# Expert stage of a hybrid transformer block: last products of a pair over all four column runs at once, 8 KB weight rows, sums in fours, gather steps behind the activation's product

## The chip, the cores and the metric

One core of a Trainium2 chip runs one program. The metric is the device time of one execution in microseconds (us); the kernel before takes 2264.77 us (median of 3 runs, 2264.67 to 2266.06).

## The reference, cut to what matters

One layer: a mixing part (convolution, neighbourhood attention, a gated recurrence), then a mixture of experts (MoE), then a norm. The change is in the MoE: 512 tokens, each sent to 2 of 32 experts, each expert with three weight matrices of 4 MiB in fp32.

```python
def _hier_moe(h, w_rg, b_rg, w_re, b_re, w1, w3, w2):
    ...
    def expert_block(args):
        e, xb = args
        return (jax.nn.silu(xb @ w1[e]) * (xb @ w3[e])) @ w2[e]

    ys = lax.map(expert_block, (blk_e, xs)).reshape(P, D)
    ys = ys * slot_w.astype(ys.dtype)[:, None]
    return jax.ops.segment_sum(ys, slot_tok, num_segments=N + 1)[:N]
```

With D = 2048 and 512 hidden columns, w1 and w3 are 2048 x 512 and w2 is 512 x 2048.

## The kernel before

The experts run in 16 **pairs** (`expert_pair`, L1444). An expert has 64 token slots, so that the two experts j of a pair stand side by side in the array: a product takes 64 of the 128 columns of TensorE (PE) for each of them, and the results fill the two halves of one PSUM bank. A fp32 matmul of the program is two rows MATMUL in the profile. Two pairs make a **group** of four experts: the first pair of a group has e divisible by 4, the second has e % 4 = 2.

A pair goes through these steps.

- `w1`, then `w3` (L1449 to L1463): four chunks c of 32 matmuls in all for each matrix, into a bank of `held`. After a chunk come other pieces of work: `run(late, 2)` after the first three chunks of w1, and `steps(...)` by the table `STEPS` (L43): in a second pair after each chunk of w3, in a first pair after the first two of w1.
- After w1, SiLU on ScalarE (ACT, L1467), a small product `pa` with slots and weights of the tokens (L1473), and the one-hot matrix `oht` on VectorE (DVE, L1482).
- After w3, DVE multiplies the two results (L1484), PE transposes (`pt`, L1488), ACT copies them out (`at`, L1490).
- The last products with w2 (`down_two`, L1511), for two column runs of 512 at a time: c = 0, 1 into `held[0:2]`, then c = 2, 3 into two banks `pd`; the weights come as tiles of 1024 columns, for each expert 4 KB of a row.
- DVE scales a run's result (`ys`, L1508), and `split` makes two parts of it (`wh` by ACT L128, `wl` by DVE L129).
- The **sums** (`combine`, L1426): for each column run c and each block t of 128 tokens two matmuls with all 128 columns (`pc<-wh`, `pc<-wl`, L1433), then one add on DVE into the output `xf` (L1440). They stand as separate pieces, one t each, in the queue `late`, and 16 pieces are run between later products, one or two at a time.

A **gather step** (L1387 to L1408) is a part of the next group's input: eight matmuls (L1398, `parts` with the one-hot `oh`), then the next input's part on ACT (L1246) and DVE (L1249); after every fourth step four activations on ACT write `hg` (L1406) out of two banks, `held[2:]`.

Every engine runs its instructions in the order in which the program emits them (the kernel is under a manual schedule), so that the order of the calls sets what waits behind what. The 8 PSUM banks are four `held` and four of the pool `bg`, from which `pc`, `pa`, `pt` and `pd` come. Weights are loaded by SyncE's queue into places of 1 MiB, as soon as a place is free (`load_weights`, L1149).

```python
STEPS = {"w3": (2, 2, 2, 2), "w2": (2, 2), "w1": (2, 2, 0, 0)}
...
        nc.vector.tensor_mul(a, gu[1], a)
        run(late, 1)
        pt = bank("pt")
        for f in range(4):
            nc.tensor.transpose(pt[:, cc(f)], a[:, cc(f)], ident)
        at = slab.tile([P, 512], F32, name="at", tag="raw", bufs=6)
        nc.scalar.copy(at, pt)
        run(late, 1)
```

Of the kernel before, what the change touches and what calls it, by code (L numbers as in the profile page):

```python
# [39 lines left out]
JOB = {"gate": 0.7, "zf": 1.4, "zb": 1.4, "k": 2.2, "q": 1.4}  # L40
NW = 6
SPLITS = {0: (4,), 1: (5,), 2: (6, 7), 4: (8,), 5: (9,), 6: (10, 11), 8: (12,), 9: (13,), 10: (14,), 11: (15,)}
STEPS = {"w3": (2, 2, 2, 2), "w2": (2, 2), "w1": (2, 2, 0, 0)}  # L43
FIRST = (6, 4, 4, 2)
BOTH = ("k", "v", "zf", "zb", "i")
HEAD = ("zf", "zb", "i", "hq", "g")
# [4 lines left out]
def hybrid_block_kernel(ctx: ExitStack, tc: tile.TileContext, I, out):  # L51
# [10 lines left out]
    def bank(name):  # L62
        return psum.tile([P, 512], F32, name=name, tag="bg")
# [58 lines left out]
    def split(w, n=512, scale=None):  # L122
        wh, wl = split_tiles(n)
        if scale:
            nc.scalar.mul(wh, w, scale)
            nc.vector.scalar_tensor_tensor(wl, w, scale, wh.bitcast(F32), op0=ALU.mult, op1=ALU.subtract)
        else:
            nc.scalar.copy(wh, w)  # L128
            nc.vector.tensor_sub(wl, w, wh.bitcast(F32))  # L129
        return wh, wl  # L130


    cs = work.tile([P, KT, 32], F32, name="cs", tag="bias", bufs=2)
# [103 lines left out]
    def run(q, n):  # L237
        for _ in range(min(n, len(q))):
            q.popleft()()
# [872 lines left out]
    wseq = deque()  # L1112

    def add(name, e, k, nk, o, n):
        v = I[name][e:e + 2].rearrange("e (k p) n -> p e k n", p=P)
        wseq.append((nk, n, v[:, :, k:k + nk, o:o + n]))
# [5 lines left out]
    for e in range(0, NE, 2):  # L1122
        for name in ("w1", "w3"):
            for c in range(4):
                for j in range(2):
                    add_run(name, e + j, c)
        if e < NE - 2:
            for c in (0, 2):
                for k in range(4):
                    add("w2", e, k, 1, 512 * c, 1024)  # L1130
            continue
        for c in range(4):
            if c < 3:
                for k in (0, 2):
                    add("w2", e, k, 2, 512 * c, 512)
            else:

                add("w2", e, 0, 4, 512 * c, 256)
                for k in (0, 2):
                    add("w2", e, k, 2, 512 * c + 256, 256)  # L1140
# [3 lines left out]
    until = {p: total for p in range(8)}  # L1144
    until[0] = 24 + 8
    for c in range(4):
        until[1 + c] = 20 + 2 * c

    def load_weights(n=1000):  # L1149
        while places and wseq and n:  # L1150
# [18 lines left out]
    def next_w(n=1):  # L1169

        places.extend(used)
        used.clear()
        load_weights()
        ws = []
        for _ in range(n):
            w, at = wtiles.popleft()
            used.append(at)
            ws.append(w)
        return ws if n > 1 else ws[0]
# [89 lines left out]
    held = [mmbank("held") for _ in range(4)]  # L1269
# [37 lines left out]
    w = tiny("w", [4, NL])  # L1307
# [61 lines left out]
    def prod():  # L1369
        turn.rotate()  # L1370
        return turn[0]

    def gather(g):

        oh = moe.tile([P, 4, 4, CAP], F32R, name="oh", tag="oh", bufs=1)
        for t in range(4):
            nc.vector.tensor_tensor(oh[:, t], iota[:, None, 1:CAP + 1].to_broadcast([P, 4, CAP]),
                                    place[:, t, 4 * g:4 * g + 4, None].to_broadcast([P, 4, CAP]), op=ALU.is_equal)
        oh = oh.rearrange("p t e s -> p t (e s)")
        hs = []  # L1380
        if g == 1:
            ob["parts"] = four(0, "parts", F32R)
        parts_ = deque(first_parts if g == 0 else [token_parts(0), token_parts(1)])
        run(lows, 1)
        yield oh, hs
        pgs = held[2:]
        for n in range(16):  # L1387
            c, t = n // 4, n % 4
            if t == 0:
                if g == 0:  # L1390
                    pgs = [bank("pg"), bank("pg")]
                pg = [pgs[i // 2][:, 256 * (i % 2):256 * (i % 2) + 256] for i in range(4)]
            if g == 0 and n < 13:
                parts_.append(token_parts(n + 3))
            now = parts_.popleft()
            for i in range(4):
                for m, y in enumerate(now):
                    nc.tensor.matmul(pg[i], y[:, cc(i)], oh[:, t], start=t == 0 and m == 0 and i % 2 == 0,  # L1398
                                     stop=t == 3 and m == 1 and i % 2 == 1)
            if g and n < 14:  # L1400
                parts_.append(token_parts(n + 2))
            if t == 3:
                for i in range(4):
                    k = 4 * c + i
                    h = moe.tile([P, 256], F32, name="hg", tag="hg", bufs=16)
                    nc.scalar.activation(h, pg[i], AF.Identity, bias=mods[:, 3, k, 1:2], scale=mods[:, 4, k, 1:2])  # L1406
                    hs.append(h)
            yield  # L1408

    xf = {}  # L1410
    late, begun = deque(), set()
# [10 lines left out]
    def steps(n):  # L1422
        for _ in range(n):
            next(coming)
# [19 lines left out]
    def expert_pair(e, oh, hs):  # L1444
        last = e == NE - 2
# [3 lines left out]
        for name in ("w1", "w3"):  # L1449
            acc = prod()  # L1450
            for c in range(4):
                if name == "w1" and e == 0:

                    steps(FIRST[c])
                ws = next_w(2)
                for k in range(4 * c, 4 * c + 4):
                    for j in range(2):
                        nc.tensor.matmul(acc[64 * j:64 * j + 64], hs[k][:, sl + 64 * j:sl + 64 * j + 64], ws[j][:, k % 4],  # L1458
                                         start=k == 0, stop=k == KT - 1, tile_position=(0, 64 * j))
                if name == "w1" and c < 3:  # L1460
                    run(late, 2)
                if ahead if name == "w3" else e and e % 4 == 0:
                    steps(STEPS[name][c])  # L1463
            gu.append(acc)
            if name == "w1":
                a = raw("act")
                nc.scalar.activation(a, acc, AF.Silu)  # L1467
                if last:
                    table(AF.Sqrt)

                pa_ = bank("pa")
                for t in range(4):
                    nc.tensor.matmul(pa_[:, 0:1 + NE], oh[:, t, sl:sl + 128].bitcast(F32), aux[:, t],  # L1473
                                     start=t == 0, stop=t == 3)
                tw = moe.tile([P, 2], F32, name="tw", tag="tw", bufs=2)
                nc.vector.tensor_copy(tw[:, 0:1], pa_[:, 0:1])
                for j in range(2):
                    nc.vector.tensor_copy(tw[64 * j:64 * j + 64, 1:2], pa_[64 * j:64 * j + 64, 1 + e + j:2 + e + j])
                if ahead:
                    gather_next(e // 4 + 1)  # L1480
                oht = slab.tile([P, T], F32R, name="oht", tag="raw", bufs=6)
                nc.vector.tensor_scalar(oht, iota[:, 0:512], tw[:, 0:1], None, op0=ALU.is_equal)  # L1482

        nc.vector.tensor_mul(a, gu[1], a)  # L1484
        run(late, 1)
        pt = bank("pt")
        for f in range(4):
            nc.tensor.transpose(pt[:, cc(f)], a[:, cc(f)], ident)  # L1488
# [16 lines left out]
        def scaled(pd, c, o, n):  # L1505

            ys = raw("ys")[:, 0:n]
            nc.vector.scalar_tensor_tensor(ys, pd, tw[:, 1:2], ga2b[:, 512 * c + o:512 * c + o + n], op0=ALU.mult, op1=ALU.mult)  # L1508
            return ys

        def down_two(c0):  # L1511

            pds = [prod(), prod()] if not c0 else [bank("pd"), bank("pd")]
            for f in range(4):
                w = next_w()
                for pd, cs in zip(pds, (slice(0, 512), slice(512, 1024))):
                    for j in range(2):
                        nc.tensor.matmul(pd[64 * j:64 * j + 64], at[:, 128 * f + 64 * j:128 * f + 64 * j + 64],  # L1518
                                         w[:, j, 0, cs], start=f == 0, stop=f == 3, tile_position=(0, 64 * j))
                if c0 and f:  # L1520
                    run(late, 2)
            return pds

        if not last:
            for c0 in (0, 2):
                pds = down_two(c0)
                if c0:
                    run(late, 2)
                if ahead:
                    steps(STEPS["w2"][c0 // 2])  # L1530
                for c, pd in zip((c0, c0 + 1), pds):
                    hl = split(scaled(pd, c, 0, 512))
                    for t in range(4):
                        late.append(lambda t=t, c=c, hl=hl: combine(oht, c, 0, 512, hl, ts=(t,)))
            return
        before = lambda ts: None
        for c, o, n in ((0, 0, 512), (1, 0, 512), (2, 0, 512), (3, 0, 256), (3, 256, 256)):
# [39 lines left out]
        for q in (2, 3):  # L1577
            nc.scalar.copy(ga2b[:, 512 * q:512 * q + 512], held[q])

    late += [gate, weights]  # L1580
    ovf = overflow()
    for g in range(NE // 4):
        now = slots
# [22 lines left out]
    with tc.If(flag > 0):  # L1606
# [15 lines left out]
        with tc.For_i(0, NE, 1) as e:  # L1622
# [8 lines left out]
            for f in range(4):  # L1631
                ws = []
# [154 lines left out]
```

## Time and profile before

| | |
|---|---|
| median of 3 runs | 2264.77 us |
| profiled execution, its own time | 2263.38 us |
| its span | 2261.5 us |
| PE busy | 2183.9 us, 97% |
| DVE, ACT, POOL busy | 54%, 31%, 12% |
| expert products with w1 and w3 | L1458, from 1236.4 to 2214.2 us |
| DMA | 600.77 MB, mean 266 GB/s |

The profiled execution's own time is 1.9 us more than its span (from the first to the last instruction); it lies 1.4 us under the median. Matmuls are pipelined and their ends are modelled, so that the busy share of PE says little; start times of successive rows say more. A row LDWEIGHTS stands under PEld.

### The profile page before, as it was taken

The page shows a single profiled execution, that of the slowest core. Times are in us where ns is not written, and L with a number is a line of the kernel's source. Part 1 is how long each engine was busy: PE and PEld are TensorE (multiplying, and loading weights), DVE is VectorE, ACT ScalarE, POOL GpSimd, SP SyncE. Part 2 cuts the span into 40 slices and gives each one's busy share as a digit, 9 for nine tenths or more (in the row PEclk, how much of TensorE's full clock was granted, in tenths as well). Part 3 has the DMA queues.
Part 4 walks back from the last instruction along what each step waited for, and adds up shares of the span by engine and source line. Part 5 has one row for each costly group of instructions (what it writes and reads, how often), then busy time and mean ns, then how long its engine had stood idle before and what let it go on. Part 6 is the DMA issues. An engine that isn't in the chain of part 4 may idle for free. (4 is left out here: it accounts for less than half of the span.)

```text
span 2261.5 us, 32139 instructions
## 1 busy us (share of the span) xinstructions
PE 2183.9 (97%) x12119; PEld 1389.6 (61%) x12119; DVE 1212.7 (54%) x2078; ACT 706.9 (31%) x1438; POOL 264.3 (12%) x320
## 2 busy tenths in 40 slices
PE   7999999999999999999999999999999999999996
PEld 4667888888877777877777344444434344444433
DVE  4478668868777676655554243434434333333435
ACT  4254232332344545343335121211203021211202
POOL 0033404405222121122000000000000000000000
PEclk9999999999999999999999999999999999999998
DMA  9964222222445655534975898999999999999996
GB/s 338 365 226 140 75 94 66 84 93 77 120 147 162 184 164 173 173 101 154 309 257 207 336 367 351 423 373 416 391 406 412 377 423 361 423 388 419 388 408 254
DMA packets 188112, 600.77 MB, mean 266 GB/s; under 512 B 21297, under 2 KB 31281, under 8 KB 155185
## 3 DMA queue, kind: packets, MB, share of 16 engines
q1 hardware_dynamic: 184112, 593.43, 70.0%
q0 software_dynamic: 3840, 5.25, 1.1%
q8 instruction: 97, 1.59, 0.3%
q14 instruction: 63, 0.51, 0.1%
HBM read 589.15 MB, written 4.19 MB: 262 GB/s over the span
## 5 line engine op out<-in xcount | busy, mean ns | idle before, releaser
L1458 PE MATMUL held<-w,hg 128*64 128x512 f32 x1848 | 462.1, 597 | 0.2 <-ACT hg L1406 0.2
L212 PE MATMUL p<-xh,wh 128*128 128x512 f32 (+1 forms) x1184 | 416.8, 365 | 2.3 <-ACT wh L128 2.1
L213 PE MATMUL p<-xl,wh 128*128 128x512 f32 (+1 forms) x1184 | 399.4, 354 | 0.0
L1458 PEld LDWEIGHTS held<-w,hg 128*64 128x64 f32 x1848 | 137.2, 136 | 253.5 <-issue 243.2
L215 PE MATMUL p<-xh,wl 128*128 128x512 f32 (+1 forms) x1184 | 254.4, 352 | 5.6 <-DVE wl L129 5.6
L129 DVE TENSOR_TENSOR wl<-w,wh 128x512 fp32r<-128x512 f32 x216 | 176.9, 819 | 150.5 <-ACT wh L128 141.0
L212 PEld LDWEIGHTS p<-xh,wh 128*128 128x128 f32 x1184 | 224.2, 189 | 43.8 <-issue 5.6
L213 PEld LDWEIGHTS p<-xl,wh 128*128 128x128 f32 x1184 | 224.0, 189 | 34.1 <-issue 1.4
L1440 DVE TENSOR_TENSOR xf<-pc,xf 128x512 f32<-128x512 f32 (+1 forms) x244 | 155.9, 676 | 154.2 <-PE pc L1433 153.2
L128 ACT CAST wh<-w 128x512 fp32r<-128x512 f32 x216 | 134.1, 621 | 312.7 <-PE p L213 226.0
L215 PEld LDWEIGHTS p<-xh,wl 128*128 128x128 f32 x1184 | 191.4, 189 | 34.9 <-DVE wl L129 7.7
L1249 DVE SCALAR_TENSOR_TENSOR parts<-xr,rst,parts 128x512 fp32r<-128x512 f32 x112 | 82.8, 750 | 168.6 <-ACT parts L1246 168.6
L388 DVE SCALAR_TENSOR_TENSOR m_acc<-w_ada,sc,m_acc 128x512 f32<-128x512 f32 x180 | 146.5, 814 | 11.3 <-DMA w_ada<-w_ada 8.9
L1246 ACT ACTIVATE parts<-xr,rst 128x512 fp32r<-128x512 f32 x112 | 80.1, 721 | 228.7 <-PE held L1398 227.9
L1398 PEld LDWEIGHTS held<-oh,parts 128*128 128x128 f32 x896 | 110.2, 188 | 30.2 <-issue 28.4
L1433 PE MATMUL pc<-wh,oht 128*128 128x512 f32 (+1 forms) x260 | 116.6, 449 | 5.3 <-DVE xf L1440 4.4
L1398 PE MATMUL held<-oh,parts 128*128 128x256 f32 x896 | 117.6, 283 | 0.0
L1433 PEld LDWEIGHTS pc<-wh,oht 128*128 128x128 f32 x260 | 48.6, 187 | 102.8 <-issue 56.0
L212 PE MATMUL po<-mx,wh 128*128 128x512 f32 x256 | 105.0, 410 | 1.7 <-ACT wh L128 1.0
L213 PE MATMUL po<-mx,wh 128*128 128x512 f32 x256 | 102.9, 402 | 0.4 <-DVE mx L1051 0.2
L1433 PE MATMUL pc<-wl,oht 128*128 128x512 f32 (+1 forms) x260 | 102.3, 394 | 0.1
L1518 PE MATMUL held<-w,at 128*64 128x512 f32 x440 | 98.1, 596 | 3.6 <-ACT at L1490 3.6
(374 smaller groups left out, 2874.3 us busy)
## 6 DMA issues: line engine op xcount, KB each, us to landing
w<-w SPq DMA_DIRECT2D x231, 1024.0 KB
w<-w SPq DMA_DIRECT2D x230, 512.0 KB
w_ada<-w_ada SPq DMA_DIRECT2D x384, 256.0 KB
w<-w_in SPq DMA_DIRECT2D x184, 256.0 KB
wm<-w SPq DMA_DIRECT2D x25, 1024.0 KB
w<-w_out SPq DMA_DIRECT2D x64, 256.0 KB
wm<-w SPq DMA_DIRECT2D x24, 512.0 KB
w_st<-w_st SPq DMA_DIRECT2D x32, 192.0 KB
```

The costliest lines, as they stand in the source:

```text
L128: nc.scalar.copy(wh, w)
L129: nc.vector.tensor_sub(wl, w, wh.bitcast(F32))
L212: nc.tensor.matmul(po, h, mh_, start=first, stop=False)
L213: nc.tensor.matmul(po, h, ml_, start=False, stop=False)
L215: nc.tensor.matmul(po, l, mh_, start=False, stop=last)
L388: nc.vector.scalar_tensor_tensor(accs[j], loads.popleft(), s, accs[j], op0=ALU.mult, op1=ALU.add)
L1249: nc.vector.scalar_tensor_tensor(l, x_, r, h.bitcast(F32), op0=ALU.mult, op1=ALU.subtract)
L1398: nc.tensor.matmul(pg[i], y[:, cc(i)], oh[:, t], start=t == 0 and m == 0 and i % 2 == 0, stop=t == 3 and m == 1 and i % 2 == 1)
L1433: nc.tensor.matmul(pc[:, 0:n], oht[:, cc(t)], y[:, 0:n], start=m == 0, stop=m == 1)
L1440: nc.vector.tensor_tensor(x_, pc[:, 0:n], x_, op=ALU.add)
L1458: nc.tensor.matmul(acc[64 * j:64 * j + 64], hs[k][:, sl + 64 * j:sl + 64 * j + 64], ws[j][:, k % 4], start=k == 0, stop=k == KT - 1, tile_ ...
L1518: nc.tensor.matmul(pd[64 * j:64 * j + 64], at[:, 128 * f + 64 * j:128 * f + 64 * j + 64], w[:, j, 0, cs], start=f == 0, stop=f == 3, tile_ ...
```

## The change

The last products of a pair run over all four column runs at once, in `held[0:4]`; each tile of w2 is now 128 full rows of one expert (8 KB each, 1 MiB in one transfer instead of two of 512 KB). The queue `late` has 7 pieces for a pair: the four sums of c = 0, the four of c = 1 with the splits of c = 2 and 3, two empty pieces, two times two sums of c = 2, the four of c = 3. One piece is run after each chunk of w1, one before and one after the transposes, one after the last products. In a second pair the last two gather steps of w3 move behind DVE's product of the activation (ahead of the transposes), two stand inside the last products, two after them; since `held[2:]` are now taken, the third quarter of the gather (`c == 2`) uses two `bg` banks. Places 1 to 4 hold weights up to tile 24 each.

```diff
-STEPS = {"w3": (2, 2, 2, 2), "w2": (2, 2), "w1": (2, 2, 0, 0)}
+STEPS = {"w3": (2, 2, 2, 0), "w2": (2, 2, 2), "w1": (2, 2, 0, 0)}
...
         if e < NE - 2:
-            for c in (0, 2):
-                for k in range(4):
-                    add("w2", e, k, 1, 512 * c, 1024)
+            for k in range(4):
+                for j in range(2):
+                    wseq.append((0, 0, I["w2"][e + j, 128 * k:128 * k + 128].rearrange("p (c n) -> p c n", n=512)))
             continue
...
-        until[1 + c] = 20 + 2 * c
+        until[1 + c] = 24
...
-                if g == 0:
+                if g == 0 or c == 2:
                     pgs = [bank("pg"), bank("pg")]
+                else:
+                    pgs = held[2:]
...
-                if name == "w1" and c < 3:
-                    run(late, 2)
+                if name == "w1":
+                    run(late, 1)
...
         nc.vector.tensor_mul(a, gu[1], a)
-        run(late, 1)
+        run(late, 4 if last else 1)
+        if ahead:
+            steps(STEPS["w2"][0])
         pt = bank("pt")
...
-        def down_two(c0):
-
-            pds = [prod(), prod()] if not c0 else [bank("pd"), bank("pd")]
+        def down_all():
+
+            pds = [prod(), prod()] + held[2:]
             for f in range(4):
-                w = next_w()
-                for pd, cs in zip(pds, (slice(0, 512), slice(512, 1024))):
+                ws = next_w(2)
+                for c, pd in enumerate(pds):
                     for j in range(2):
                         nc.tensor.matmul(pd[64 * j:64 * j + 64], at[:, 128 * f + 64 * j:128 * f + 64 * j + 64],
-                                         w[:, j, 0, cs], start=f == 0, stop=f == 3, tile_position=(0, 64 * j))
-                if c0 and f:
-                    run(late, 2)
+                                         ws[j][:, c], start=f == 0, stop=f == 3, tile_position=(0, 64 * j))
+                if ahead and f == 1:
+                    steps(STEPS["w2"][1])
             return pds
+        def some(c, hl, ts):
+            late.append(lambda: combine(oht, c, 0, 512, hl, ts=ts))
         if not last:
-            for c0 in (0, 2):
-                pds = down_two(c0)
-                if c0:
-                    run(late, 2)
-                if ahead:
-                    steps(STEPS["w2"][c0 // 2])
-                for c, pd in zip((c0, c0 + 1), pds):
-                    hl = split(scaled(pd, c, 0, 512))
-                    for t in range(4):
-                        late.append(lambda t=t, c=c, hl=hl: combine(oht, c, 0, 512, hl, ts=(t,)))
+            pds = down_all()
+            ys, hl = [], []
+            for c, pd in enumerate(pds):
+                ys.append(scaled(pd, c, 0, 512))
+                if c == 0:
+                    hl.append(split(ys[0]))
+            run(late, 1)
+            if ahead:
+                steps(STEPS["w2"][2])
+            hl.append(split(ys[1]))
+            def second():
+                combine(oht, 1, 0, 512, hl[1])
+                hl[2:] = [split(y) for y in ys[2:]]
+            some(0, hl[0], range(4))
+            late.append(second)
+            late.append(lambda: None)
+            late.append(lambda: None)
+            late.append(lambda: combine(oht, 2, 0, 512, hl[2], ts=(0, 1)))
+            late.append(lambda: combine(oht, 2, 0, 512, hl[2], ts=(2, 3)))
+            late.append(lambda: combine(oht, 3, 0, 512, hl[3]))
             return
...
-    late += [gate, weights]
+    late += [gate, weights] + [lambda: None] * 5
```

Three places show how the instructions move. The first is PE at the end of the last products of the pair e = 6, a second pair (`pd`, `held`: the results; `w`: weights; `pc`: sums; the numbers tell buffers apart). Before:

```order
L1518 MATMUL pd_13775<-w_13628,at_13711 64x512 x2
L1518 MATMUL pd_13776<-w_13628,at_13711 64x512 x2
L1433 MATMUL pc_13789<-wh_13765,oht_13547 128x512
L1433 MATMUL pc_13789<-wl_13766,oht_13547 128x512
L1433 MATMUL pc_13793<-wh_13765,oht_13547 128x512
L1433 MATMUL pc_13793<-wl_13766,oht_13547 128x512
L1518 MATMUL pd_13775<-w_13659,at_13711 64x512 x2
L1518 MATMUL pd_13776<-w_13659,at_13711 64x512 x2
L1433 MATMUL pc_13803<-wh_13765,oht_13547 128x512
```

and now:

```order
L1522 MATMUL held_12173<-w_13601,at_13655 64x512
L1522 MATMUL held_12173<-w_13603,at_13655 64x512
L1435 MATMUL pc_13747<-wh_13447,oht_13228 128x512
L1435 MATMUL pc_13747<-wl_13448,oht_13228 128x512
L1435 MATMUL pc_13751<-wh_13447,oht_13228 128x512
L1435 MATMUL pc_13751<-wl_13448,oht_13228 128x512
L1435 MATMUL pc_13755<-wh_13447,oht_13228 128x512
L1435 MATMUL pc_13755<-wl_13448,oht_13228 128x512
L1435 MATMUL pc_13759<-wh_13447,oht_13228 128x512
L1435 MATMUL pc_13759<-wl_13448,oht_13228 128x512
L1400 MATMUL pg_13689<-oh_13486,parts_12778 128x256 x4
L1400 MATMUL pg_13690<-oh_13486,parts_12778 128x256 x4
```

The sums no longer part the products of single f; four of them stand after the last product, ahead of two gather steps whose two `pg` banks come from the same pool as the `pc`.

The second is DVE in a second pair, from the low parts of the gather steps during w3 (L1249) on. Before:

```order
L1249 SCALAR_TENSOR_TENSOR parts<-xr,rst,parts 128x512 x8
L1484 TENSOR_TENSOR act<-held,act 128x512
L1440 TENSOR_TENSOR xf<-pc,xf 128x512 x2
L1249 SCALAR_TENSOR_TENSOR parts<-xr,rst,parts 128x512 x2
L1508 SCALAR_TENSOR_TENSOR ys<-held,tw,ga2b 128x512
L129 TENSOR_TENSOR wl<-ys,wh 128x512
```

and now:

```order
L1249 SCALAR_TENSOR_TENSOR parts<-xr,rst,parts 128x512 x6
L1486 TENSOR_TENSOR act<-held,act 128x512
L1442 TENSOR_TENSOR xf<-pc,xf 128x512 x2
L1249 SCALAR_TENSOR_TENSOR parts<-xr,rst,parts 128x512 x2
L1442 TENSOR_TENSOR xf<-pc,xf 128x512 x2
L1249 SCALAR_TENSOR_TENSOR parts<-xr,rst,parts 128x512 x2
L1512 SCALAR_TENSOR_TENSOR ys<-held,tw,ga2b 128x512
L129 TENSOR_TENSOR wl<-ys,wh 128x512
L1512 SCALAR_TENSOR_TENSOR ys<-held,tw,ga2b 128x512 x3
L1442 TENSOR_TENSOR xf<-pc,xf 128x512 x4
```

Two low parts have moved from ahead of the activation's product to behind it; four scalings and one split stand ahead of the adds of the last four sums.

The third is ACT around the copy of the transposes (`at`) in a second pair. Now:

```order
L1246 ACTIVATE parts<-xr,rst 128x512 x4
L1408 ACTIVATE hg<-held,mods 128x256 x4
L1494 COPY at<-pt 128x512
L1246 ACTIVATE parts<-xr,rst 128x512 x2
```

Before, the same four rows stand there (L1406 and L1490 in place of L1408 and L1494): here nothing has moved on ACT, while on PE the transposes now follow the gather steps at once.

## Rows read from the trace of the kernel before

**Rows 1.** The page's 40 slices: busy tenths of the DMA engines.
```profile
DMA  9964222222445655534975898999999999999996
```
**Rows 2.** Stretches: us; busy (count) PE, PEld, DVE, ACT, POOL; PEclk, DMA share, GB/s.
```profile
1300.00:2200.00 900.00, 878.59 (x4275) 388.68 (x4271) 341.34 (x559) 183.15 (x311) 0.00 (x0) 1.00 0.98 395
1552.00:1572.00 20.00, 20.00 (x92) 7.66 (x90) 8.43 (x18) 3.05 (x5) 0.00 (x0) 1.00 1.01 426
1518.00:1534.00 16.00, 15.56 (x74) 5.49 (x72) 1.98 (x3) 0.58 (x1) 0.00 (x0) 1.00 1.01 352
```
**Rows 3.** DMA view of the stretch 1518 to 1534 us.
```profile
DMA packets 1542, 5.63 MB, mean 352 GB/s; under 512 B 170, under 2 KB 170, under 8 KB 1541
```
**Rows 4.** Waits of PE and PEld, 1240 to 2215 us: us in total, times, longest.
```profile
PE pt L1488 <- DVE act L1484: 14.7, 15, 1.8
...
PEld held L1518 <- DMA w<-w: 4.0, 14, 0.3
```
**Rows 5.** Timeline of PE: starts of two groups' first pair (start, length).
```profile
1619.08 3.22 PE L1458 MATMUL held<-w,hg 128*64 128x512 f32 x14
...
1745.22 1.08 PE L1458 MATMUL held<-w,hg 128*64 128x512 f32 x4
```
**Rows 6.** Timeline of PE: sums between the last products of a second pair.
```profile
1731.02 3.65 PE L1518 MATMUL pd<-w,at 128*64 128x512 f32 x16
1734.60 0.50 PE L1433 MATMUL pc<-wh,oht 128*128 128x512 f32 x1
1734.94 0.39 PE L1433 MATMUL pc<-wl,oht 128*128 128x512 f32 x1
1735.17 0.40 PE L1433 MATMUL pc<-wh,oht 128*128 128x512 f32 x1
...
1735.73 1.94 PE L1518 MATMUL pd<-w,at 128*64 128x512 f32 x8
1737.60 0.50 PE L1433 MATMUL pc<-wh,oht 128*128 128x512 f32 x1
```
**Rows 7.** Timeline of PE: from w3 to the last products, first pair.
```profile
1655.48 0.50 PE L1433 MATMUL pc<-wh,oht 128*128 128x512 f32 x1
...
1657.77 0.65 PE L1518 MATMUL held<-w,at 128*64 128x512 f32 x2 [0.21 <-ACT at L1490]
```
**Rows 8.** Timeline of PE: from the last products to the next w1, first pair.
```profile
1674.21 0.50 PE L1433 MATMUL pc<-wh,oht 128*128 128x512 f32 x1
...
1676.98 3.65 PE L1458 MATMUL held<-w,hg 128*64 128x512 f32 x16
```
**Rows 9.** Timeline of PE: from w3 to the last products, second pair.
```profile
1710.61 2.14 PE L1398 MATMUL held<-oh,parts 128*128 128x256 f32 x16
1712.67 3.65 PE L1458 MATMUL held<-w,hg 128*64 128x512 f32 x16
1716.26 2.15 PE L1398 MATMUL held<-oh,parts 128*128 128x256 f32 x16
...
1721.94 5.37 PE L1518 MATMUL held<-w,at 128*64 128x512 f32 x24 [0.22 <-ACT at L1490]
```
**Rows 10.** Timelines of DVE and ACT there.
```profile
1719.86 0.69 DVE L1484 TENSOR_TENSOR act<-held,act 128x512 f32<-128x512 f32 x1
...
1718.95 1.91 ACT L1406 ACTIVATE hg<-held,mods 128x256 f32<-128x256 f32 x4
1721.30 0.58 ACT L1490 COPY at<-pt 128x512 f32<-128x512 f32 x1 [0.44 <-PE pt L1488]
```
**Rows 11.** Timeline of PE: start of the sums that end a second pair.
```profile
1740.59 0.50 PE L1433 MATMUL pc<-wh,oht 128*128 128x512 f32 x1
```
**Rows 12.** Timeline of DVE: scaling, split and adds after the last products.
```profile
1664.08 0.75 DVE L1508 SCALAR_TENSOR_TENSOR ys<-held,tw,ga2b 128x512 f32<-128x512 f32 x1 [5.78 <-PE held L1518]
1665.57 0.69 DVE L129 TENSOR_TENSOR wl<-ys,wh 128x512 fp32r<-128x512 f32 x1 [0.74 <-ACT wh L128]
...
1674.97 1.29 DVE L1440 TENSOR_TENSOR xf<-pc,xf 128x512 f32<-128x512 f32 x2 [1.70 <-PE pc L1433]
```

## Prediction

> **What bounds the kernel now.** I read the page first. Its slices show the DMA engines nearly full for the last third of the span [rows 1], which is the expert stage, so the first question is whether weights or PE set its pace. From 1300 to 2200 us PE is busy for 878.59 of 900 us and the DMA engines for 0.98 of the time, at 395 GB/s [rows 2]; both are near their end. The waits decide: in the last products, where the weights are shortest, PE's weight loads wait for DMA in 14 places for 4.0 us in all, never over 0.3 us, while its transposes alone wait 14.7 us for DVE [rows 4]. So PE sets the pace and the weights arrive just in time. A group takes 1745.22 - 1619.08 = 126.14 us [rows 5]. PE's granted clock is 1.00, its upper level, in all these stretches [rows 2]. What is left to win is PE time that is not a matmul's own, read from the starts of successive rows.
>
> **What parting the products costs.** Sixteen narrow products (64 columns, L1518) take 1734.60 - 1731.02 = 3.58 us to the next start, eight take 1737.60 - 1735.73 = 1.87 us [rows 6]. Eight more cost 1.71, so one costs 0.214 and a stretch has a fixed 0.16 us. The four matmuls of two sums take 1735.73 - 1734.60 = 1.13 us, and inside follow each other by 1735.17 - 1734.94 = 0.23 [rows 6]: 4 x 0.23 = 0.92, fixed 0.21. To part narrow products by sums thus costs 0.37 us beyond the work.
>
> [...]
>
> **The change, part by part.** In the order of PE's matmuls the narrow products stand in 158 unbroken stretches before and 112 now (the first and the last pair of all included: six fewer in each full group). The number of matmuls is the same. 46 x 0.37 = **17.0 us less**.
>
> *First pairs, w3 to the last products.* 1657.77 - 1655.48 = 2.29 us [rows 7], of which four sum matmuls are 0.92, the fixed part 0.21, and four transposes at most 0.46. That last is an estimate from the gather matmuls: sixteen take 1712.67 - 1710.61 = 2.06 us with the fixed part [rows 9], 0.116 each, and a transpose has half their columns. That leaves 0.70 us idle. Now four sum matmuls stand before and four behind the transposes: 1.13 us cover the product of 0.69 us, and 0.92 us the copy of 0.58 us [rows 10] with its start. I take the idle time as gone: 7 x 0.70 = **4.9 us less**. The bounds are none and all of it.
>
> *First pairs, end.* Eight sum matmuls take 1676.98 - 1674.21 = 2.77 us [rows 8], their work is 8 x 0.23 + 0.21 = 2.05; 0.72 us is a wait for banks that DVE's adds give back. Now four sums find four free banks. Seven first pairs and the very first: 8 x 0.72 = **5.8 us less**.
>
> *Second pairs, w3 to the last products.* 1721.94 - 1716.26 = 5.68 us [rows 9]; the work is 2.06 + 0.92 + 0.46 = 3.44, idle 2.24. DVE starts the activation's product at 1719.86 [rows 10], 3.60 us after w3's last product, because two low parts of the gather stand ahead of it on DVE. The change puts it first. But the next wait in line is ACT's: its four `hg` begin 1718.95 - 1716.26 = 2.69 us after the two gather steps begin, take 1.91, and the copy of 0.58 us stands behind them [rows 9, 10]; this order on ACT is not changed. With four sum matmuls (1.13 us) now ahead of the gather, the last products start 1.13 + 2.69 + 1.91 + 0.58 = 6.31 us after w3. The work there is 3.44 + 0.92 = 4.36, so 1.95 us stay idle: 7 x 0.29 = **2.0 us less**. Most of the stall stays, with ACT as its cause.
>
> *Second pairs, end.* Today 1745.22 - 1740.59 = 4.63 us [rows 5, 11] for work of 2.05 + 1.85 = 3.90, idle 0.73. Now the four sums find two free banks only, since the gather holds two of the pool; the third sum waits for DVE's add of the first. On DVE that add stands behind the scaling of all four runs and one split. The first run is complete 12 products, 2.57 us, before the end; DVE starts about 0.3 later (an estimate: 28 products after 1657.77 is 1663.76, and the scaling of rows 12 starts at 1664.08), the split 1665.57 - 1664.08 = 1.49 after that [rows 12], and it takes 0.69 and three scalings 0.75 each, a little less where they overlap: the adds begin some 2.0 us after the last product. An add takes 1.29 / 2 = 0.65 us [rows 12]. So the third sum starts at about 2.7, the fourth at 3.3, it ends at 3.8, and the two gather steps add 1.9: 5.7 us, idle 1.8. 7 x (1.8 - 0.73) = **7.5 us more**. Nothing in the rows shows this wait itself; its ends are no wait (a gain of 5 us) and, if the third sum had to wait for all four adds, 2.6 us more for each pair (18 us). I take 1.8, since each term has a row.
>
> *Weights.* 8 KB packets alone move at 426 GB/s, the w2 rows of 4 KB at 352, both at a full DMA share of 1.01 [rows 2, 3]. A group's 48 tiles of 1 MiB are 50.3 MB, 118 us at 426. Today a share of 0.98 in 126.14 us means some 122 us of transfers. PE's group becomes 126.14 - 22.2 / 7.75 = 123.3 us, so both with and without faster rows the weights keep under it. No term of the sum, but the faster rows are the cover for all the others.
>
> [...]
>
> *At nothing.* The seven empty pieces at the start, the places until tile 24, one transfer in place of two: all lie under PE's work in a stage where PE rarely waits for a tile [rows 4].
>
> **The sum.** 17.0 + 4.9 + 5.8 + 2.0 - 7.5 = 22.2 us less. The span of 2261.5 becomes 2239.3, the profiled execution's 2263.38 becomes 2241.2, and as that lies 1.4 under the median of 2264.77, I predict **2242.6 us**.
>
> **The rivals.**
>
> *Parting is cheap, so joining wins little.* [...] Chance 0.10. [...]
>
> *The second pairs lose nothing.* If neither ACT's order nor the banks bind, 1.95 + 1.8 us come back seven times, 26 us, and the time is 2216. The order on ACT speaks against it. Chance 0.06.
>
> *The weights set the pace.* If the share of 0.98 [rows 2] is all that the queue can do and w2's slow rows have another cause than their length, PE's savings turn into waits for DMA: no change, 2264.8. Against it are the short waits [rows 4] and 426 GB/s held for 20 us. Chance 0.05.
>
> *Slower: first pairs run dry.* A first pair now needs 25.2 MB in 57.9 - 2.5 = 55.4 us (1676.98 - 1619.08 [rows 5, 8], less its terms), and 426 GB/s brings that in 59.1. The shortage of 3.7 us must come out of tiles loaded ahead in the second pair. If the free places do not allow this lead, PE waits 3.7 us in eight first pairs: 29.6 - 22.2 = 7.4 slower, 2272. It decides from a wait of 2.8 us for each. Against it: the same pair has a shortage today too, 57.9 us against 59.1 and more with the slow rows, without waits. Chance 0.05.
>
> **How the numbers follow.** The forecast has the remaining 0.74, with a range of its own of 2230 to 2250 from the bounds of the second pairs. With the first rival this is 0.84, and the range is 2229 to 2256. Within 0.2% (4.5 us, about what a measurement of this kernel can tell from no change) is the third rival, 0.05; slower is the fourth, 0.05; faster is the rest, 0.90.
>
> **What would show it.** Right: eight sum matmuls in 2.05 us after a first pair's last products; a first pair near 55.4 us and a second near 67.9; in second pairs `at` starting directly behind `hg`, and 5.7 us from the last product to w1; single waits for tiles still under a us. Wrong: second pairs longer than the 68.2 of today by more than 3 us, waits of PE for `w` in first pairs, or a fixed part that stays although the stretches are fewer.

## The result, and the profile after

The changed kernel takes 2239.99 us (median of 4 runs, 2237.02 to 2242.75), the kernel before beside it 2264.72: a ratio of 0.9891 with an interval of 0.9876 to 0.9905. That is 24.7 us less, where 22.2 were forecast. The profiled execution took 2239.92 us for a span of 2238.1. Ratios here use fast runs alone (those not over 1.5% above the shortest of their kernel): every run below is one, but for two of the four with lower and upper halves.

From the page of the changed kernel: the busy times.

```profile
span 2238.1 us, 31980 instructions
...
PE 2160.3 (97%) x12119; PEld 1397.9 (62%) x12119; DVE 1205.9 (54%) x2078; ACT 705.0 (31%) x1438; POOL 263.9 (12%) x320
```

PE's share is 97% as before, so the shares don't show the gain; the starts of rows do. Most of the expert stage as one stretch (the columns of [rows 2]):

```profile
1300.00:2170.00 870.00, 849.88 (x4243) 395.39 (x4241) 334.87 (x555) 180.53 (x309) 0.00 (x0) 1.00 0.98 406
```

The same weights now come at 406 GB/s where [rows 2] has 395, at the same share of 0.98: that the queue is "busy" says little about how fast it moves.

PE's timeline in one group: the starts of its first pair (w1, L1460), of the sums after w3 (L1435), of the last products (L1522), of the sums behind them, and of the second pair.

```profile
1606.74 1.08 PE L1460 MATMUL held<-w,hg 128*64 128x512 f32 x4
...
1643.64 0.50 PE L1435 MATMUL pc<-wh,oht 128*128 128x512 f32 x1
...
1644.67 0.60 PE L1492 MATMUL pt<-cf,act 128*128 128x128 f32 x4
1645.03 0.48 PE L1435 MATMUL pc<-wh,oht 128*128 128x512 f32 x1
...
1646.13 3.23 PE L1522 MATMUL held<-w,at 128*64 128x512 f32 x14
...
1660.02 0.50 PE L1435 MATMUL pc<-wh,oht 128*128 128x512 f32 x1
...
1662.06 1.51 PE L1460 MATMUL held<-w,hg 128*64 128x512 f32 x6
```

The first pair takes 1662.06 - 1606.74 = 55.32 us. From w3 to the last products it needs 1646.13 - 1643.64 = 2.49 us with eight sum matmuls, where [rows 7] needs 2.29 with four: the idle time is gone. The eight at its end take 1662.06 - 1660.02 = 2.04 us, where [rows 8] have 2.77.

The second pair of that group, from w3 to the last products, and from those to the next w1, on PE:

```profile
1701.91 0.50 PE L1435 MATMUL pc<-wh,oht 128*128 128x512 f32 x1
...
1702.93 2.04 PE L1400 MATMUL held<-oh,parts 128*128 128x256 f32 x16
1704.81 0.60 PE L1492 MATMUL pt<-cf,act 128*128 128x128 f32 x4
...
1707.96 2.79 PE L1522 MATMUL held<-w,at 128*64 128x512 f32 x12 [1.63 <-ACT at L1494]
...
1724.06 0.50 PE L1435 MATMUL pc<-wh,oht 128*128 128x512 f32 x1
...
1726.39 0.50 PE L1435 MATMUL pc<-wh,oht 128*128 128x512 f32 x1 [1.13 <-DVE xf L1442]
...
1727.55 2.03 PE L1400 MATMUL pg<-oh,parts 128*128 128x256 f32 x16
1729.51 1.08 PE L1460 MATMUL held<-w,hg 128*64 128x512 f32 x4
```

It takes 1729.51 - 1662.06 = 67.45 us, the group 122.77 (126.14 before). Both forecast waits stand there, for ACT and for DVE. What those two engines do meanwhile:

```profile
1705.52 1.91 ACT L1408 ACTIVATE hg<-held,mods 128x256 f32<-128x256 f32 x4
1707.31 0.59 ACT L1494 COPY at<-pt 128x512 f32<-128x512 f32 x1
```

```profile
1702.05 0.69 DVE L1486 TENSOR_TENSOR act<-held,act 128x512 f32<-128x512 f32 x1 [2.23 <-PE held L1460]
...
1723.67 2.06 DVE L1512 SCALAR_TENSOR_TENSOR ys<-held,tw,ga2b 128x512 f32<-128x512 f32 x3
1725.65 1.28 DVE L1442 TENSOR_TENSOR xf<-pc,xf 128x512 f32<-128x512 f32 x2
```

The activation's product is ready at 1702.74 and the transposes follow at 1704.81, yet their copy waits until `hg` is through at ACT. At the end DVE's adds begin only behind three scalings. Over the whole stage these are PE's waits (us in total, times, longest):

```profile
PE held L1522 <- ACT at L1494: 12.0, 8, 1.6
PE pc L1435 <- DVE xf L1442: 6.8, 6, 1.1
PE pc L1435 <- DVE xf L1440: 1.7, 2, 1.5
PE pt L1492 <- DVE act L1486: 0.9, 1, 0.9
...
PE held L1460 <- DMA w<-w: 0.5, 1, 0.5
```

and the largest of the waits of its weight loads (PEld) for a tile:

```profile
PEld held L1460 <- DMA w<-w: 1.5, 2, 1.3
```

In the kernel before, ACT's copy and DVE's adds already had PE wait, for less:

```profile
PE pc L1433 <- DVE xf L1440: 4.4, 14, 0.3
PE held L1518 <- ACT at L1490: 3.6, 15, 0.7
```

The 14.7 us of transposes that wait for DVE [rows 4] have become 0.9, and 12.0 + 8.5 us stand at the two new places; waits of these two kinds were 3.6 and 4.4 before. So PE's waits in the stage come to much the same sum: in these rows 14.7 + 4.4 + 3.6 = 22.7 us before, 12.0 + 6.8 + 1.7 + 0.9 + 0.5 = 21.9 now. By these rows hardly anything is won; the gain shows in the starts alone. A first pair's end, for one, lost 0.72 us by its starts before, and its wait is given as 0.3.

### The profile page after: what moved, and what is told of

Its sections match the earlier page's. It is cut to its first block, busy times and chain, and to the rows that moved or that the text cites. A ratio compares the mean times of both kernels' runs of the same rounds, so it can differ in the third digit from the quotient of the medians.

```text
span 2238.1 us, 31980 instructions
## 1 busy us (share of the span) xinstructions
PE 2160.3 (97%) x12119; PEld 1397.9 (62%) x12119; DVE 1205.9 (54%) x2078; ACT 705.0 (31%) x1438; POOL 263.9 (12%) x320
## 5 line engine op out<-in xcount | busy, mean ns | idle before, releaser
L1460 PE MATMUL held<-w,hg 128*64 128x512 f32 x1848 | 459.3, 596 | 0.7 <-DMA w<-w 0.5
L1460 PEld LDWEIGHTS held<-w,hg 128*64 128x64 f32 x1848 | 138.5, 137 | 257.9 <-issue 244.8
L1522 PE MATMUL held<-w,at 128*64 128x512 f32 x872 | 210.8, 594 | 12.0 <-ACT at L1494 12.0
L1442 DVE TENSOR_TENSOR xf<-pc,xf 128x512 f32<-128x512 f32 (+1 forms) x244 | 151.1, 675 | 60.1 <-PE pc L1435 58.5
L1249 DVE SCALAR_TENSOR_TENSOR parts<-xr,rst,parts 128x512 fp32r<-128x512 f32 x112 | 83.5, 751 | 154.8 <-ACT parts L1246 154.8
L1522 PEld LDWEIGHTS held<-w,at 128*64 128x64 f32 x872 | 66.4, 137 | 143.3 <-issue 124.2
L128 ACT CAST wh<-ys 128x512 fp32r<-128x512 f32 x60 | 37.1, 618 | 264.2 <-DVE ys L1512 134.0
L1435 PE MATMUL pc<-wh,oht 128*128 128x512 f32 (+1 forms) x260 | 110.7, 427 | 8.5 <-DVE xf L1442 6.8
L1512 DVE SCALAR_TENSOR_TENSOR ys<-held,tw,ga2b 128x512 f32<-128x512 f32 (+1 forms) x65 | 45.4, 737 | 117.0 <-PE held L1522 108.1
L1435 PE MATMUL pc<-wl,oht 128*128 128x512 f32 (+1 forms) x260 | 101.4, 391 | 0.1
```

The lines of the kernel that those rows point to most:

```text
L1249: nc.vector.scalar_tensor_tensor(l, x_, r, h.bitcast(F32), op0=ALU.mult, op1=ALU.subtract)
L1435: nc.tensor.matmul(pc[:, 0:n], oht[:, cc(t)], y[:, 0:n], start=m == 0, stop=m == 1)
L1442: nc.vector.tensor_tensor(x_, pc[:, 0:n], x_, op=ALU.add)
```

## The experiments

My theory: PE's own time sets the pace; joining the narrow products won 0.35 to 0.37 us for each stretch, and ACT's order and the banks took a part back in second pairs. Rivals: parting is cheap and the gain has another source; the faster weight rows are what the gain rests on; moving the gather steps is what won.

**The last sums of first pairs parted again.** In first pairs the four sums that stand behind the last products go one by one behind f = 0, 1, 2 and the end: three more stretches in each, the same matmuls.

```diff
+                if not ahead and f < 3:
+                    run(late, 1)
...
-            late.append(lambda: combine(oht, 3, 0, 512, hl[3]))
+            for ts in [range(4)] if e % 4 == 0 else [(0,), (1,), (2,), (3,)]:
+                late.append(lambda ts=ts: combine(oht, 3, 0, 512, hl[3], ts=ts))
```

> The changed kernel with the last four sums of seven first pairs parted again: one behind each of the first three f of the last products and one at the end, where all four stood. The work is the same, three narrow and three wide stretches are added in each of these pairs. At 0.37 us for each that is 7 x 3 x 0.37 = 7.8 us, about 2248, a first pair taking 55.33 + 1.11 = 56.4 us. [...]

Measured: 2246.54 us (2244.74 to 2248.84), 6.6 more than the changed kernel. PE's timeline in the parted kernel, start of a first pair and a part of its end:

```profile
1610.85 1.08 PE L1460 MATMUL held<-w,hg 128*64 128x512 f32 x4
...
1662.32 0.50 PE L1435 MATMUL pc<-wh,oht 128*128 128x512 f32 x1
...
1666.57 0.50 PE L1435 MATMUL pc<-wh,oht 128*128 128x512 f32 x1
...
1667.23 1.08 PE L1460 MATMUL held<-w,hg 128*64 128x512 f32 x4
```

The pair takes 1667.23 - 1610.85 = 56.38 us where the changed kernel takes 55.32, with no wait in these rows. That is 1.06 for three stretches, **0.35 us for one**. Six of the seven pairs grow by 1.05 to 1.07 us, the earliest by 0.64. Had parting cost nothing, the pair would have stayed at 55.32. The runs' median lies 1.5 us under the 2248 expected from 0.37 for each; the pair decides. Only first pairs were parted; the same price for second pairs is taken over from them.

**The gather steps alone moved,** in the kernel before: two of them go behind DVE's product of the activation, nothing else is changed.

```diff
-STEPS = {"w3": (2, 2, 2, 2), "w2": (2, 2), "w1": (2, 2, 0, 0)}
+STEPS = {"w3": (2, 2, 2, 0), "w2": (2, 2, 2), "w1": (2, 2, 0, 0)}
...
         run(late, 1)
+        if ahead:
+            steps(STEPS["w2"][0])
         pt = bank("pt")
...
-                    steps(STEPS["w2"][c0 // 2])
+                    steps(STEPS["w2"][1 + c0 // 2])
```

> The kernel before, with one part of the change alone: in second pairs the last two gather steps of w3 stand behind DVE's product of the activation, ahead of the transposes. By the prediction's reading DVE's wait ends and ACT's takes its place: one sum (0.21 + 0.46 us), then gather, hg and copy, 0.67 + 2.69 + 1.91 + 0.58 = 5.85 us where 5.68 stood, so nothing is won: 0 to 2 us over the time before. If the place of the gather steps is what matters, the idle 2.24 us go: 7 x 2.24 = 15.7 us less than before.

Measured: 2266.79 us, a ratio of 1.0002 (0.9992 to 1.0012) to the kernel before. Its waits of PE:

```profile
PE held L1520 <- ACT at L1492: 16.7, 15, 2.1
PE pc L1433 <- DVE xf L1440: 4.5, 14, 0.3
PE pt L1490 <- DVE act L1484: 2.5, 8, 0.9
```

The wait for DVE falls from 14.7 us [rows 4] to 2.5, and the waits for ACT's copy, 3.6 us before, grow to 16.7: together 18.3 before and 19.2 now. The last instruction in the chain has another name, and the time is the same. This part of the change by itself wins nothing.

**The second pairs' two waits taken away.** First the sums: those that end a second pair stand behind f = 1 instead, ahead of the two gather steps there.

```diff
                 if ahead and f == 1:
+                    run(late, 1)
                     steps(STEPS["w2"][1])
...
-            run(late, 1)
             if ahead:
                 steps(STEPS["w2"][2])
+            else:
+                run(late, 1)
```

> The changed kernel with one move: in second pairs the four last sums stand inside the last products, directly ahead of the two gather steps that are there already, and no longer behind the last product. If DVE's queue (four scalings and a split ahead of the add that frees a bank) and the two banks that the gather holds make the stretch of 5.45 us at the end of a second pair, that end shrinks to the two gather steps alone (2.07 us), the middle stretch grows from 2.07 by 8 x 0.23 = 1.86, and 5.45 - 2.07 - 1.86 = 1.5 us are won in each of seven second pairs: 10.6 us, about 2229. If the sums are slow there for another reason (their matmuls themselves, the weights), the middle stretch grows by 3.4 us instead and the time stays near 2240.

Measured: 2231.14 us (2229.94 to 2231.34), a ratio of 0.9845 (0.9828 to 0.9861), 8.9 less than the changed kernel. PE's timeline of such a pair from its sums on:

```profile
1711.25 0.50 PE L1435 MATMUL pc<-wh,oht 128*128 128x512 f32 x1
...
1713.20 2.03 PE L1400 MATMUL pg<-oh,parts 128*128 128x256 f32 x16
1715.16 7.09 PE L1522 MATMUL held<-w,at 128*64 128x512 f32 x32
1722.18 2.13 PE L1400 MATMUL pg<-oh,parts 128*128 128x256 f32 x16
```

Eight sum matmuls run without a wait (1.95 us to the gather), and no row has an idle time any more.

Then the copy: in second pairs the transposes and ACT's copy stand ahead of the gather steps.

```diff
-        if ahead:
-            steps(STEPS["w2"][0])
         pt = bank("pt")
...
         nc.scalar.copy(at, pt)
+        if ahead:
+            steps(STEPS["w2"][0])
         run(late, 1)
```

> The changed kernel with one move: in second pairs the transposes and ACT's copy of them stand ahead of the two gather steps, so that the copy is no longer behind four hg activations. If ACT's order makes the idle time there (6.05 us for 4.4 us of work), the stretch shrinks to about 4.4 us and 7 x 1.65 = 11.6 us are won, less some 0.15 us a pair because the third column run writes a bank that hg must leave first: about 2229. If the products wait for their weights at that place instead, they wait as long as before and the time stays near 2240.

Measured: 2228.61 us (2227.56 to 2229.74), a ratio of 0.9835 (0.9818 to 0.9851), 11.4 less than the changed kernel. PE and ACT there:

```profile
1697.38 0.60 PE L1490 MATMUL pt<-cf,act 128*128 128x128 f32 x4
1697.74 2.12 PE L1400 MATMUL held<-oh,parts 128*128 128x256 f32 x16
...
1700.70 4.08 PE L1522 MATMUL held<-w,at 128*64 128x512 f32 x17
```

```profile
1698.02 0.59 ACT L1492 COPY at<-pt 128x512 f32<-128x512 f32 x1 [4.54 <-PE pt L1490]
...
1700.41 1.91 ACT L1408 ACTIVATE hg<-held,mods 128x256 f32<-128x256 f32 x4
```

The copy now precedes `hg`, and gather and sums cover it. So the forecast cause of each wait is the cause: with that taken away, each wait goes. For the sums two things were forecast together, DVE's order and the two banks that the gather holds; the one move ends both, and which of them weighs more was not parted.

**Both moved.**

> Both moves together. If PE alone sets the pace, the gains add up: 22 us, about 2218, a group then taking 122.8 - 3.2 = 119.6 us. The weights of a group need 50.3 MB / 426 GB/s = 118.1 us, so if the weights are the next limit, first waits of PE for tiles w appear in first pairs and the time stays some us above 2218; if the weights set the pace already, nothing is won beyond 2240.

Measured: 2217.13 us (2215.44 to 2218.47), a ratio of 0.9782 (0.9766 to 0.9799): 22.9 less than the changed kernel, where the two gains by themselves are 8.9 and 11.4. In the traces they add up: the second pair of this group, from w1 to w1, takes 67.45 us in the changed kernel, 65.92 and 65.80 with one move each, and 64.24 with both, 3.21 less for 1.53 + 1.65. This version beats both kernels, by 2.2% and by 1.0%. Most of its expert stage as one stretch:

```profile
1300.00:2150.00 850.00, 849.51 (x4261) 397.42 (x4259) 335.00 (x559) 182.85 (x311) 0.00 (x0) 1.00 1.00 417
```

PE starts a group at 1596.53, its second pair at 1651.87 and the next group at 1716.11:

```profile
1596.53 0.65 PE L1460 MATMUL held<-w,hg 128*64 128x512 f32 x2
...
1651.87 1.51 PE L1460 MATMUL held<-w,hg 128*64 128x512 f32 x6
...
1716.11 1.08 PE L1460 MATMUL held<-w,hg 128*64 128x512 f32 x4
```

119.58 us for a group, in which PE uses 50.3 MB of weights, 421 GB/s. At the 426 GB/s of [rows 2] they would take 118.1 us: by that estimate 1.5 us are left before the weights set the pace, which no run here tried.

**Are the 8 KB rows needed?** The tiles of w2 are loaded in two transfers of 512 KB with rows of 4 KB, first in the changed kernel, then in the version with both moved.

```diff
+                elif two:
+                    for h in (0, 2):
+                        nc.sync.dma_start(w[:, h:h + 2], v[:, h:h + 2])
```

> The changed kernel with its tiles of w2 loaded as before the change: two transfers of 512 KB for a tile, with 4 KB of each row. The order on every other engine stays. The changed kernel's group takes 55.33 + 67.46 = 122.8 us on PE. If the 122 us of transfers in a group that the prediction read from the share of 0.98 hold, the weights stay just under PE and the time stays within 2240 to 2244. If 352 GB/s holds for all of w2, a group's weights need 78.8 + 47.7 = 126.4 us, PE waits for tiles, and the time is 2240 + 7.5 x 3.6 = 2267.

> The kernel with both moves (2217.1 us, a group of 119.6 us on PE) with the same 4 KB rows of w2. By 122.4 us of transfers in a group the weights are now over PE: 7.5 x 2.8 = 21 us more, about 2238, with waits of PE for tiles; by 126.4 us it is 7.5 x 6.8 = 51 us, 2268. If the length of the rows does not matter, 2217.

Measured: 2242.78 us (ratio 0.9901, 0.9885 to 0.9918) and 2219.46 (0.9803, 0.9787 to 0.982): 2.8 and 2.3 us more than with 8 KB rows, with intervals that overlap those of whole rows: a small cost, at the edge of what the times can tell. The traces tell more. By the starts of w1, each pair but the last takes the same time with either length, within 0.1 us; from the start of the last pair to the end it is 1.35 and 1.69 us more, and there PE waits for one tile for 1.4 us, where it waits 0.5 and 0.7 with 8 KB rows. The second kernel's stretch and its packets:

```profile
1300.00:2150.00 850.00, 849.52 (x4259) 397.52 (x4257) 334.95 (x558) 183.29 (x311) 0.00 (x0) 1.00 1.01 416
```

```profile
DMA packets 64674, 353.86 MB, mean 416 GB/s; under 512 B 7180, under 2 KB 7180, under 8 KB 35852
```

More than half of its packets are under 8 KB, and it moves 416 GB/s where whole rows move 417. At most 2.8 of the 24.7 us rest on the rows' length. The same could have been read in the kernel before, in another stretch of 4 KB rows than the one of [rows 2]:

```profile
1834.00:1846.00 12.00, 10.98 (x64) 5.89 (x60) 3.67 (x6) 5.40 (x11) 0.00 (x0) 1.00 1.03 418
1896.00:1914.00 18.00, 17.57 (x84) 6.11 (x82) 1.98 (x3) 0.58 (x1) 0.00 (x0) 1.00 0.96 325
```

Rows of 4 KB came at 418 GB/s in the one and at 325 in the other. What slows the second kind (the stretch of [rows 3] is one) I did not try; it is not the packets' size. Loaded as in the second run, where the two transfers of a tile bring the two halves of the same rows and not the same columns of two experts, rows of 4 KB have no such stretch: from 1406 us on, no slice of 21 us lies under 402 GB/s, where the kernel before goes down to 320. Whether it is that difference was not tried.

**8 KB rows in two transfers.** To tell the number of transfers from the length of rows, each w2 tile of the best version comes in two transfers of 64 partitions, with full rows: first the lower and the upper half, then the even and the odd partitions.

```diff
+                    for h in (0, 64):
+                        nc.sync.dma_start(w[h:h + 64], v[h:h + 64])
```

```diff
-                    for h in (0, 64):
-                        nc.sync.dma_start(w[h:h + 64], v[h:h + 64])
+                    for h in (0, 1):
+                        nc.sync.dma_start(w[h::2], v[h::2])
```

> The kernel with both moves and two transfers of 512 KB for a tile of w2, but split by partitions, so that every row keeps its 8 KB. If the length of the rows makes the weights fast, the time is that of the kernel with both moves (2217); if the size or number of the transfers does, it is that of the same kernel with 4 KB rows.

> Both idle times moved as before, and each w2 tile in two transfers of 64 partitions and 8 KB rows, now the even partitions and the odd ones in place of the lower and the upper half. [...] Rival: a transfer of 64 rows is slow whichever partitions it writes; then 2490 us again at about 327 GB/s. Rival: the alternate rows of w2 make the reading slower; then anything above 2230 with packets longer than in the halves.

Measured: the halves 2494.32 us, with four runs from 2461.19 to 2550.43; the ratio of the two shortest (2461.19 and 2486.14) is 1.0919 (1.0854 to 1.0984), against both expectations; even and odd 2217.54 (2215.25 to 2219.29), a ratio of 0.9787 (0.9771 to 0.9804), as with whole tiles. The stretch of the kernel with halves (a run of 2502.51 us), and the largest of PE's waits in it (us, times, longest):

```profile
1300.00:2150.00 850.00, 737.17 (x3287) 328.31 (x3285) 261.82 (x432) 143.62 (x244) 0.00 (x0) 0.94 1.01 327
```

```profile
PE held L1525 <- DMA w<-w: 77.2, 36, 4.1
```

and the stretch with even and odd partitions:

```profile
1300.00:2150.00 850.00, 849.50 (x4257) 396.92 (x4253) 336.54 (x557) 181.54 (x310) 0.00 (x0) 1.00 1.00 417
```

Both have as many transfers of the same size, with 64 rows of 8 KB. So it is not the number of transfers or of partitions that costs, but which partitions one of them writes, or which rows of w2 it reads for them: the edit moves both together. Only w2's tiles, a third of the weights, come so, and 327 GB/s is the mean with the whole tiles; if the whole tiles moved at the 426 of [rows 2], those in halves moved at some 223, an estimate from these two speeds. With halves the granted clock was 0.94 on the mean of this stretch, with even and odd partitions 1.00. How much of the loss is the clock's was not separated.

## Why the prediction was right, and where it was not

The predicted 2242.6 us is 2.6 over the measured 2239.99. By its steps, each with what the trace of after has in its place:

| step | predicted | measured |
|---|---|---|
| parting, 46 stretches | 0.37 each, 17.0 less | 0.35 each (parted run, first pairs), 16.1 less |
| first pairs, w3 to last products, 7 | 0.70, 4.9 less | 2.29 + 0.92 - 2.49 = 0.72, 5.0 less |
| first pairs' end, 8 | 0.72, 5.8 less | 2.77 - 2.04 = 0.73, 5.8 less |
| second pairs, w3 to last products, 7 | 0.29, 2.0 less | 5.68 + 0.92 - 6.05 = 0.55, 3.9 less |
| second pairs' end, 7 | 1.07, 7.5 more | 5.45 - 4.63 = 0.82, 5.7 more |
| sum | 22.2 less | 25.1 less |

The median fell by 24.7 and the span by 2261.5 - 2238.1 = 23.4. By the starts of w1 rows the 23.4 are: the first pairs behind the very first 17.9 less, the seven second pairs behind them 5.0 less, the very first pair 6.2 less (61.56 to 55.38), from the start of the last pair to the end 5.0 more (79.91 to 84.90), and a stage that begins 0.7 later. The very first pair and the last one differ so much because eight sums, 16 x 0.23 = 3.7 us of work, no longer run in the very first pair and are added to the last; the prediction has no word of this, and it cancels. The 1.7 us between the measured terms and the span are the later start, the second pair of the first group, which wins 0.2 us where its terms give 1.1, and small differences elsewhere.

The two terms for second pairs miss by 1.9 and 1.8 us to the same side. That the time came closer than they did is in part luck: parting was taken 0.9 us too large, and the 1.7 us go the same way.

*Parting* held, and the parted run puts the price at the stretch itself. The rival by which it is cheap falls. The upper end of 2256 us in the forecast's range supposes a far lower price, which no run shows; the parted run shows 0.35 us for a stretch.

*Second pairs* had the right mechanisms and terms that were some 0.26 us too large. `at` starts directly behind `hg`, as forecast, but the chain of 1.13 + 2.69 + 1.91 + 0.58 = 6.31 measured 1.02 + 2.59 + 1.79 + 0.65 = 6.05: I added durations, where on PE and ACT a next start lies a little ahead of the end that the row gives (1702.93 is 1.02 after 1701.91; the copy starts 1.79 after `hg`). At the end the third sum starts 1726.39 - 1724.06 = 2.33 us after the last product in place of 2.7, in the main for the same reason: DVE's three scalings take 1725.65 - 1723.67 = 1.98 us from start to start, where 2.25 were added. The rival by which second pairs lose nothing falls: PE waited 20.5 us for ACT and DVE in the stage (12.0 + 8.5), and the two moves together won 22.9.

*Weights* is the step that failed, though it carried no term. I read "a share of 0.98 in 126.14 us means some 122 us of transfers" (0.98 x 126.14 is 123.6; 122.4 against a full share of 1.01), and called the faster rows "the cover for all the others". By that reading 119.58 us for a group were not to be had with 4 KB rows; the second run with such rows shows 2219.46 us, and they are: 119.5 us for a group. The share says that something is in flight, not how fast the queue could go: it was 0.98 at 395 GB/s and at 406, and is 1.01 at 327 with halves. And one stretch with 352 GB/s [rows 2, 3] was taken for the speed of 4 KB rows, where other stretches of that trace have 418. The two rivals in which the weights bind fall with the waits: PE waits once for a tile in the whole stage, for 0.5 us, and first pairs don't run dry. The waits of weight loads that I read as 4.0 us were one row of four, 9.1 us in all, none over 0.4; now they are 1.8 from 1240 to 2195 us. One sign is missed: single waits were to stay under a us, and in the last pair one weight load waits 1.3.

## What to carry to other kernels

Count the unbroken stretches of each shape of matmul, and price a stretch from the starts of rows in runs of different lengths; that price held to 0.02 us in all but one of the pairs where it was tried. When work is moved out of the way of one wait, follow the chain on every engine up to the next wait in line: here a move alone won nothing, because ACT's order took DVE's place, and two more moves of a few lines won another 1%. A queue's busy share is no measure of what it has left (here it was 1.01 at 327 GB/s and at 426): compare its speed in several stretches with the highest one seen.

## What the runs showed of the hardware that I had not expected

- With w2's tiles, a third of the weights, in two transfers of 64 neighbouring partitions, the queue moved 327 GB/s in the expert stage at a share of 1.01 and down to 210 in slices of 21 us; with two transfers of 64 even and 64 odd partitions it moved 417, as with one of 128. Which partitions a transfer writes and which rows of w2 it reads changed together; which of the two it is, no run separated.
- In the kernel with both moved, a weight row of 4 KB cost next to nothing against 8 KB: 416 against 417 GB/s at shares of 1.01 and 1.00, and a wait of 1.4 us in place of 0.7 in the last pair.
- One core held 417 GB/s for 850 us in the kernel with both moved.
